# Seven block products for eight in the second projections of a hybrid encoder step, values included

## The chip, the cores and the metric

The kernel runs on one core of a Trainium2 chip. The metric is the device time of one execution in microseconds (us). TensorE (PE) multiplies matrices into PSUM banks; VectorE (DVE), ScalarE (ACT) and GpSimd (POOL) work on tiles in SBUF and PSUM; SyncE (SP) issues DMA transfers. Each engine takes its own instructions in order and waits on semaphores for the others.

## The reference

One inference step of a two-layer streaming encoder on 2048 prompt tokens and 32 sampled tokens (2080 rows, 1024 channels). Layer A is a gated delta rule with its output projection and a layer norm. Its result h goes into the second projections: shared keys and values, queries and gates. Layer B is sliding-window attention with sinks over two earlier chunks of 64 and the own one, gated, projected and normed.

```python
def shared_kv(h, w_kv, pos):
    b, l, _ = h.shape
    kv = h @ w_kv          # 256 key and 256 value channels; the keys are rotated
...
proj = h @ w_in            # 1024 query and 1024 gate channels; the queries are rotated
...
x1 * cos - x2 * sin, x2 * cos + x1 * sin   # on 16 of the 64 channels of a head
```

All products are computed to nearly float32 accuracy from two parts of each operand: hi is the value rounded to the fast matmul format (fp32r), lo = value - hi, and a product is hi x hi + hi x lo + lo x hi.

## The kernel before

The program runs, in order: the projections of layer A, the delta rule, the output projection of layer A (O1, 17 tiles of 128 tokens, which writes h and its transpose hT to DRAM and is in part mixed into the delta rule), the second projections (class P2), and attention with layer B's output projection and norm. This document is about P2, which lies from about 1290 to 1781 us, and the first iterations of attention, which follow.

P2 cuts the 2080 tokens into five blocks of TB = 416 and the channels into tiles ("slabs") of 128. Weights are the stationary operand, activations the moving one. For a slab and a block, `project` issues 24 matmuls of 128x416 into one bank: eight k of 128 input channels by the three hi/lo pairs. Eighteen slabs are projected so: two of keys, eight of queries, eight of gates (z). A slab's weights are loaded by SP (512 KB), rounded to w_hi by ACT, and the rest w_lo is made by POOL (128x1024, line 56). An activation block is loaded in four parts, rounded by ACT (line 70) and its lo made by POOL or DVE (line 71), once for the whole stage; all five blocks stay in SBUF.

Values are computed the other way round, with tokens as stationary operand, since attention wants tokens on partitions: `value_tile` takes 17 tiles of tokens with 24 matmuls of 256 columns each (lines 1389 to 1391).

`rotated` does keys and queries. After each of its 50 blocks come a copy by ACT (line 1345), a stream shuffle by DVE (1346), the product with the sines by POOL (1347) and two DVE operations (1348, 1349). The cosines and sines of all tokens stay in SBUF. Beside it, `keep_out_weights` splits layer B's output weights part by part (lines 1089 to 1093) and stores both parts in DRAM for attention. `gate` makes z/2 and tanh(z/2) on ACT (1430, 1431) and (tanh + 1) z/2 on DVE (1432).

Six or more PSUM banks serve P2 in turn, so that a bank comes free long before it is written again. In P2 only PE's and DVE's order is written by hand, in its first part; the rest is scheduled from the order of the code. Eight gates of blocks 0 and 1 are kept for the start of attention: sixteen halves of twelve matmuls that fill PE's pauses there (`gates`, line 2054 on). Attention takes the score tiles of the prompt in the order 14 to 31, then 0 to 13.

Of the kernel before, what the change touches and what calls it, by code (L numbers as in the profile page):

```python
# [11 lines left out]
F32 = mybir.dt.float32  # L12
# [9 lines left out]
D = 1024  # L22
# [1057 lines left out]
def keep_out_weights(nc, pool, src, kept):  # L1080


    w = D // 2
    last = None
    for k in range(KC):
        for c in (slice(0, w), slice(w, D)):
            t = pool.tile([128, 2, w], F32R, tag="wo_parts", name="wo_parts")
            raw = t[:, 1].bitcast(F32)
            nc.sync.dma_start(raw, src[k][:, c])
            if last:  # L1090
                nc.sync.dma_start(*last)
            nc.scalar.copy(t[:, 0], raw)
            nc.gpsimd.tensor_tensor(out=t[:, 1], in0=raw, in1=t[:, 0], op=ALU.subtract)
            last = kept[:, k, :, c].rearrange("a p d -> p a d"), t[:].bitcast(F32)
            yield
    nc.sync.dma_start(*last)
    yield


# [192 lines left out]
class P2:  # L1292
# [3 lines left out]
    def __init__(self, tc, right, spare, I, O, T):  # L1296
        self.tc, self.nc, self.I, self.O, self.T = tc, tc.nc, I, O, T
        self.resr = new_pool(tc, right, "p2_resr", 1, side="right")
        self.wp = new_pool(tc, right, "p2_w", 2, side="right")
        self.wk = new_pool(tc, right, "p2_wk", 3, side="right")  # L1300
        self.front = ExitStack()
        self.resf = new_pool(tc, self.front, "p2_resf", 1, side="right")
        self.stg = new_pool(tc, spare, "p2_stg", 2, side="right")
        self.ppr = new_pool(tc, spare, "p2_psr", 2, PSUM, side="right")
        self.ppl = None
        self.turn = 0
        self.x = {}
        self.w = {}

    def load_right(self):  # L1310
        for b in (0, 1):
            self.load(b, (self.resf, self.resr)[b])

    def open_left(self, left):
        self.resl = new_pool(self.tc, left, "p2_resl", 1, side="left")
        self.wo = new_pool(self.tc, left, "p2_wo", 2, side="left")
        self.ppl = new_pool(self.tc, left, "p2_psl", 6, PSUM, side="left")
        for b in (2, 3, 4):
            self.load(b, self.resl)

    def load(self, b, res):
        nc = self.nc
        raws = []
        for q in range(4):
            raw = self.stg.tile([128, 2, TB], F32, tag="act_raw", name="act_raw")
            s = slice(q * 2, q * 2 + 2)
            (nc.sync if q % 2 == 0 else nc.scalar).dma_start(
                raw[:], self.T["hT"][s, :, b * TB:(b + 1) * TB].rearrange("h p t -> p h t"))
            raws.append((s, raw[:]))
        self.x[b] = split_acts(nc, res, b, raws, nc.gpsimd if b < 3 else nc.vector)  # L1330

    def ps(self):
        self.turn += 1
        pool = self.ppr if self.ppl is None or self.turn % 4 == 0 else self.ppl
        return pool.tile([128, 512], F32, tag="ps", name="ps")

    def right_ps(self):
        return self.ppr.tile([128, 512], F32, tag="ps", name="ps")

    def rope(self, ps, b, scale):  # L1340
        nc, V = self.nc, self.nc.vector
        ts = slice(b * TB, b * TB + TB)
        a = self.wk.tile([128, TB], F32, tag="ra", name="ra")
        s = self.wk.tile([128, TB], F32, tag="rs", name="rs")
        nc.scalar.activation(a[:], ps, AF.Copy, scale=scale)
        V.stream_shuffle(s[:], a[:], [(i + 8) % 16 if i < 16 else i for i in range(32)])  # L1346
        nc.gpsimd.tensor_tensor(out=s[:], in0=s[:], in1=self.sin[:, ts], op=ALU.mult)  # L1347
        V.tensor_tensor(out=a[:], in0=a[:], in1=self.cos[:, ts], op=ALU.mult)
        V.tensor_tensor(out=a[:], in0=a[:], in1=s[:], op=ALU.add)
        return a  # L1350

    def values(self):
        nc = self.nc
        vh = self.resl.tile([128, KC, 256], F32R, tag="cos", name="vh")
        vl = self.resl.tile([128, KC, 256], F32R, tag="sin", name="vl")
        for i in range(2):
            ks = slice(i * 4, i * 4 + 4)
            vr = self.wp.tile([128, 4, 256], F32, tag="w_raw", name="vr", bufs=1)
            nc.scalar.dma_start(vr[:], self.I["w_v"][:, ks, :])
            nc.scalar.copy(vh[:, ks], vr[:])  # L1360
            nc.gpsimd.tensor_tensor(out=vl[:, ks], in0=vr[:], in1=vh[:, ks], op=ALU.subtract)
        full = TB // 128 * 128
        rows = TB - full
        eh, el = (self.wo.tile([128, 2, D // 2], F32R, tag="wo_parts", name="x_rest")[:].rearrange(
            "p a (b t) -> p (a b) t", t=128) for _ in range(2))
        for b in range(NB - 1):
# [28 lines left out]
    def rotated(self):  # L1395
# [6 lines left out]
        for i in range(10):  # L1402
            w = split_weights(nc, self.wp, I["w_k"][i] if i < 2 else I["b_w_in"][i - 2], nc.gpsimd)
            for b in range(NB):
                if b % 2 == 0:
                    next(beside, None)
# [843 lines left out]
```

## Time and profile before

| | |
|---|---|
| median of the 3 runs shown | 2108.95 us (2107.36 to 2113.84) |
| span of the profiled execution | 2109.4 us |
| PE busy | 2075.3 us, 98% |
| DVE, ACT, POOL busy | 1308.9, 902.1, 833.9 us |
| bytes moved by DMA | 307.78 MB, 146 GB/s |

Share of the span says how much of the time an engine had something to do. The chain that ended last is followed back from the last instruction, at each step to what released it; a share there says what the end depended on. A window's row lists, for a stretch of the span, the busy time of each engine with its instructions, the clock that PE was granted (1.00 is full speed), the share of time in which the 16 DMA engines were busy, and GB/s. A row of the timeline gives start and duration, engine, line, operation, out<-in with their shapes, and in brackets the idle time before and what ended it. A group's row of one line ends with "busy us, mean ns of one | idle time before them".

### The profile page before, as it was taken

The numbers are of one execution on the slowest core, as the hardware profiler recorded it, in microseconds if no ns is written. First come the engines' busy times: TensorE is split into PE (matmuls) and PEld (weight loads), VectorE is DVE, ScalarE is ACT, GpSimd is POOL, SyncE is SP. The second block draws the span as 40 slices with busy tenths as digits, with TensorE's granted clock in tenths as the row PEclk, the third lists the DMA queues.
The fourth block names the chain that finished last, engine by engine and source line by source line (L and its number), as shares of the span: only waits on it lengthen the run. The fifth ranks groups of instructions, "written<-read, shape, count | busy, mean of one in ns | idle before, by whom it ended". The sixth has DMA issues, their size and how long they took to land.

```text
span 2109.4 us, 37222 instructions
## 1 busy us (share of the span) xinstructions
PE 2075.3 (98%) x14062; PEld 1910.6 (91%) x14062; DVE 1308.9 (62%) x2450; ACT 902.1 (43%) x2266; POOL 833.9 (40%) x1180
## 2 busy tenths in 40 slices
PE   8999999999999999999999999999999999999998
PEld 6999999999999999999888888999999997777775
DVE  4676676666557688889977886214544214666665
ACT  4444444445632377667752212312111225555552
POOL 1422222222132187778830201226443103566665
PEclk9999999999999999999999999999999999999999
DMA  5222332346665545556746764546212249534321
GB/s 206 71 62 87 106 111 93 95 127 207 196 195 156 179 157 179 163 169 209 267 162 200 227 213 121 159 154 230 90 66 82 67 109 317 141 101 121 101 72 65
DMA packets 263779, 307.78 MB, mean 146 GB/s; under 512 B 71424, under 2 KB 194624, under 8 KB 263328
## 3 DMA queue, kind: packets, MB, share of 16 engines
q1 hardware_dynamic: 252816, 282.30, 42.8%
q10 hardware_dynamic: 10784, 23.11, 3.3%
q8 instruction: 111, 1.82, 0.4%
q14 instruction: 68, 0.56, 0.1%
HBM read 189.11 MB, written 116.60 MB: 145 GB/s over the span
## 4 chain that ended last, share of the span: by engine, by line
PE 91%; DVE 3%; DMA 2%; POOL 2%; ACT 1%; issue 1%; SPq 0%; DVEq 0%; ACTq 0%; POOLq 0%
PE ps L79 17%; PE ps L81 17%; PE ps L80 17%; PE ot L1146 3%; PE ot L1147 3%; PE ot L1148 3%; PE po L1146 3%; PE po L1148 3%; PE po L1147 3%; PE S L1706 2%; PE ot L1739 2%; PE tr L1721 2%; PE g L695 1%; PE gq L831 1%; PE ks L846 1%; PE sp L846 1%
## 5 line engine op out<-in xcount | busy, mean ns | idle before, releaser
L79 PE MATMUL ps<-act_hi,w_hi 128*128 128x416 f32 x1936 | 682.6, 353 | 0.5 <-ACT act_hi L70 0.4
L81 PE MATMUL ps<-act_hi,w_lo 128*128 128x416 f32 x1936 | 681.4, 352 | 0.0
L80 PE MATMUL ps<-act_lo,w_hi 128*128 128x416 f32 x1936 | 678.4, 350 | 0.5 <-DVE act_lo L71 0.4
L79 PEld LDWEIGHTS ps<-act_hi,w_hi 128*128 128x128 f32 x1936 | 363.9, 188 | 5.3 <-ACT act_hi L70 1.2
L80 PEld LDWEIGHTS ps<-act_lo,w_hi 128*128 128x128 f32 x1936 | 363.7, 188 | 5.5 <-DVE act_lo L71 1.2
L81 PEld LDWEIGHTS ps<-act_hi,w_lo 128*128 128x128 f32 x1936 | 363.4, 188 | 3.7 <-DVE w_lo L56 0.4
L56 POOL TENSOR_TENSOR w_lo<-w_raw,w_hi 128x1024 fp32r<-128x1024 f32 x43 | 115.3, 2682 | 477.3 <-ACT w_hi L55 449.2
L209 DVE SCALAR_TENSOR_TENSOR y<-R,convw,y 128x2083 f32<-128x2083 f32 x72 | 182.9, 2542 | 63.8 <-ACT y L206 47.8
L1540 POOL TENSOR_TENSOR P<-e,sm 128x384 f32<-128x384 f32 (+2 forms) x128 | 101.1, 811 | 170.9 <-DVE sm L1530 164.6
L729 POOL TENSOR_TENSOR tm<-L,Tt 128x60 f32<-128x60 f32 (+19 forms) x365 | 133.6, 366 | 81.2 <-issue 40.1
L731 POOL TENSOR_TENSOR Tt<-Tt,tm 128x60 f32<-128x60 f32 (+19 forms) x365 | 138.7, 380 | 28.6
L1526 ACT ACTIVATE e<-S,nm 128x193 f32<-128x193 f32 (+2 forms) x260 | 104.6, 415 | 95.7 <-DVE nm L1521 58.1
L305 ACT COPY R<-ps 128x416 f32<-128x416 f32 (+1 forms) x144 | 60.2, 442 | 106.8 <-PE ps L81 96.0
L1146 PE MATMUL po<-wo_hi,g_hi 128*128 128x512 f32 x256 | 103.6, 405 | 1.0 <-DVE r L1154 0.8
L1146 PE MATMUL ot<-wo,g_hi 128*128 128x512 f32 x256 | 103.7, 405 | 0.0
L1347 POOL TENSOR_TENSOR rs<-rs,sin 128x416 f32<-128x416 f32 x50 | 70.6, 1412 | 78.8 <-DVE rs L1346 72.6
L1147 PE MATMUL ot<-wo,g_hi 128*128 128x512 f32 x256 | 101.2, 395 | 0.0
L1148 PE MATMUL ot<-wo,g_lo 128*128 128x512 f32 x256 | 101.0, 394 | 0.0
L1148 PE MATMUL po<-wo_hi,g_lo 128*128 128x512 f32 x256 | 100.2, 392 | 0.6 <-DVE g_lo L1189 0.6
L1147 PE MATMUL po<-wo_lo,g_hi 128*128 128x512 f32 x256 | 99.9, 390 | 0.0
L55 ACT CAST w_hi<-w_raw 128x1024 fp32r<-128x1024 f32 x47 | 49.4, 1050 | 108.4 <-PE ps L80 74.3
L1432 DVE SCALAR_TENSOR_TENSOR za<-zs,za 128x416 f32<-128x416 f32 x40 | 31.7, 796 | 102.3 <-ACT za L1431 102.1
(301 smaller groups left out, 3917.9 us busy)
## 6 DMA issues: line engine op xcount, KB each, us to landing
w_raw<-in_w_in SPq DMA_DIRECT2D x40, 512.0 KB
w_raw<-in_b_w_in SPq DMA_DIRECT2D x19, 512.0 KB
k<-s_k SPq DMA_DIRECT2D x17, 512.0 KB
E<-s_E SPq DMA_DIRECT2D x17, 512.0 KB
s_bz<-za SPq DMA_DIRECT2D x40, 208.0 KB
s_bq<-ra SPq DMA_DIRECT2D x40, 208.0 KB
s_q<-y SPq DMA_DIRECT2D x8, 1024.0 KB
s_wo<-wo_parts SPq DMA_DIRECT2D x16, 512.0 KB
```

What stands on the lines that cost most here:

```text
L56: sub.tensor_tensor(out=lo[:], in0=raw[:], in1=hi[:], op=ALU.subtract)
L79: nc.tensor.matmul(ps, hi[:, k, :], xh[:, k, :], start=(k == 0), stop=False)
L80: nc.tensor.matmul(ps, hi[:, k, :], xl[:, k, :], start=False, stop=False)
L81: nc.tensor.matmul(ps, lo[:, k, :], xh[:, k, :], start=False, stop=(k == KC - 1))
L209: nc.vector.scalar_tensor_tensor(out=y[:], in0=R[:, j:j + W], scalar=self.convw[:, i, j:j + 1], in1=y[:], op0=ALU.mult, op1=ALU.add)
L729: P.tensor_tensor(out=tm[:n, i0 - k:, :w], in0=L[:n, i0:, j:j + 1].to_broadcast(sh), in1=Tt[:n, j:j + 1, :w].to_broadcast(sh), op=ALU.mult)
L731: P.tensor_tensor(out=Tt[:n, i0:, :w], in0=Tt[:n, i0:, :w], in1=tm[:n, i0 - k:, :w], op=ALU.subtract)
L1146: nc.tensor.matmul(ps[:n], ghi[:, k, :n], hi, start=a, stop=False)
L1147: nc.tensor.matmul(ps[:n], ghi[:, k, :n], lo, start=False, stop=False)
L1148: nc.tensor.matmul(ps[:n], glo[:, k, :n], hi, start=False, stop=z)
L1526: self.nc.scalar.activation(x.e[:, h, u, :x.n], x.S[:, h, u, :], AF.Exp, bias=x.nm[:, h, u:u + 1], scale=1.0, accum_out=x.sm[:, h, u:u + 1])
L1540: self.nc.gpsimd.tensor_tensor(out=x.P[:, u, :nj * 128].rearrange("r (j h k) -> r j h k", h=2, k=64), in0=x.e[:, :, u, :n].rearrange("r h ...
```

## The change

The second projections are regrouped into 20 feature tiles in ten pairs: keys 0 and 1, values 2 and 3, queries 4 to 11, gates 12 to 19. Block 0 is multiplied as before, but in two products of four k each ("singles", twelve matmuls). Blocks 1 and 2, then blocks 3 and 4, are taken as a 2 x 2 matrix of blocks (halves of k by the two blocks) against 2 x 2 weights (tiles i and i+1 by halves of k), with seven products P1 to P7 of twelve matmuls instead of eight (Winograd's form).

- The seven activation operands b11, b21, t2, t1, t3, t4, b22 are made by `build`, once for each pair of blocks: per k four loads of 208 KB, four sums on POOL, seven roundings on ACT and seven subtractions on DVE. It takes three of its steps after each product while singles run, and what is left before the first paired product.
- The weight operands r1, r2, s1, s2 and two differences are made by `sevens` with four POOL sums per tile pair; each operand of 128x512 is rounded by ACT, and its lo is made by DVE (by POOL until O1 ends). A product's weights are made four products ahead and fetched eight ahead, in a ring of eight slots.
- The sums of products stand in PSUM: P1, then P6, P7 and P4 add up in bank X (two buffers; copied by ACT at each step), P2 in Y, P5 then P3 in Z (one buffer each). DVE adds Y and Z to the copies (line 1447).
- Values come as feature tiles and are turned on PE by 40 transposes (`turn`).
- Weight columns are arranged so that the rotated channels lie in tiles 0, 4 and 8 alone: 15 rotations. Cosines and sines are loaded for each (cs, 416 KB, one buffer). Rows are put back in order by a store to a DRAM scratch (`rows`) and copies from there.
- `out_weights` takes a part of layer B's output weights every seven paired products, with one buffer.
- Every engine's order is now written by hand after O1. Attention takes its tiles from 8 on instead of 14, and has fourteen products of gates (tiles 13 to 19 of block 0) as filler. `LATE` becomes 5.

```diff
+    def part(self, raw, hi, lo, sub):
+        self.nc.scalar.copy(hi, raw)
+        sub.tensor_tensor(out=lo, in0=raw, in1=hi, op=ALU.subtract)
...
+    def sevens(self, raws):
+        r1, r2 = raws
+        a, b = slice(0, 4), slice(4, 8)
+        P = self.nc.gpsimd
+        yield self.operand(r1[:, a])
+        yield self.operand(r1[:, b])
+        s1, s2 = (self.sums.tile([128, 4, 128], F32, tag=t, name=t) for t in ("s1", "s2"))
+        P.tensor_tensor(out=s1[:], in0=r2[:, a], in1=r2[:, b], op=ALU.add)
+        P.tensor_tensor(out=s2[:], in0=s1[:], in1=r1[:, a], op=ALU.subtract)
+        yield self.operand(s2[:])
+        yield self.operand(s1[:])
...
+        for k in range(4):
+            def part(name, raw, sub):
+                self.part(raw[:], x[name][0][:, k, :], x[name][1][:, k, :], sub)
+            b11, b12, b22, b21 = (self.raw_act(i, b) for i, b in ((k, c), (k, d), (4 + k, d), (4 + k, c)))
+            part("b11", b11, nc.vector)
+            yield
+            P.tensor_tensor(out=b11[:], in0=b12[:], in1=b11[:], op=ALU.subtract)
+            part("b21", b21, nc.vector)
+            yield
+            part("b22", b22, nc.vector)
+            P.tensor_tensor(out=b12[:], in0=b22[:], in1=b12[:], op=ALU.subtract)
+            yield
+            P.tensor_tensor(out=b22[:], in0=b22[:], in1=b11[:], op=ALU.subtract)
+            part("t1", b11, nc.vector)
+            yield
+            P.tensor_tensor(out=b21[:], in0=b21[:], in1=b22[:], op=ALU.subtract)
+            part("t2", b22, nc.vector)
...
+        steps = {"P1": ("b11", "X", True, lambda: copied("X", "p1")),
+                 "P2": ("b21", "Y", True, lambda: self.finish(added("Y", "p1"), i, c)),
+                 "P6": ("t2", "X", False, lambda: copied("X", "u2")),
+                 "P5": ("t1", "Z", True, None),
+                 "P7": ("t3", "X", False, after7),
+                 "P4": ("t4", "X", False, lambda: self.finish(copied("X", "c"), i + 1, c)),
+                 "P3": ("b22", "Z", False, lambda: self.finish(added("Z", "u2"), i, d))}
...
+            if last:
+                out += [g["P1"], last["P4"], g["P2"], last["P3"]]
+            else:
+                out += [g["P1"], g["P2"]]
+            out += [g["P6"], g["P5"], g["P7"]]
...
+        early = [*singles(first, self.ps), *one, between[0], a4, between[1], a3, *between[2:], *two, last[0], b4, last[1], b3]
+        late = singles(range(self.Z + 1, self.Z + 8), late_ps)
...
+            if products[p].paired:
+                drain(self.side)
+                next(self.beside, None)
+            yield from self.multiply(products[p])
+            if products[p].after:
+                products[p].after()
+            for _ in range(self.STEPS):
+                next(self.side, None)
...
+        cs = self.tab.tile([128, 2, TB], F32, tag="cs", name="cs")
+        nc.sync.dma_start(cs[:], self.I["cs"][b])
+        s = self.out()
+        V.stream_shuffle(s[:n], a[:n], [(i + 8) % 16 + i // 16 * 16 for i in range(32)])
+        nc.gpsimd.tensor_tensor(out=s[:n], in0=s[:n], in1=cs[:n, 1, :], op=ALU.mult)
+        V.tensor_tensor(out=a[:n], in0=a[:n], in1=cs[:n, 0, :], op=ALU.mult)
+        V.tensor_tensor(out=a[:n], in0=a[:n], in1=s[:n], op=ALU.add)
...
-        order = list(range(14, 32)) + list(range(14))
+        order = list(range(8, 32)) + list(range(8))
```

In the rows below the changed kernel's lines have its own numbers. The first place is right after O1. On POOL there stood, before, the lo parts of block 2, the value weights and the first slabs of keys:

```order
L71 TENSOR_TENSOR act_lo2_13727<-act_raw_13722,act_hi2_13726 128x832
L71 TENSOR_TENSOR act_lo2_13727<-act_raw_13724,act_hi2_13726 128x832
L1370 COPY x_rest_14001<-act_lo2_13727 128x8x32
L1361 TENSOR_TENSOR vl_13991<-vr_13996,vh_13990 128x1024
L1370 COPY x_rest_14001<-act_lo3_13745 128x8x32
L56 TENSOR_TENSOR w_lo_14496<-w_raw_14493,w_hi_14495 128x1024
```

On POOL now stand the sums of the first build (lines 1372 to 1381, one set of four for each k) and the weight sums s1 and s2 of the first pair:

```order
L1372 TENSOR_TENSOR act_raw_13859<-act_raw_13861,act_raw_13859 128x416
L1376 TENSOR_TENSOR act_raw_13861<-act_raw_13863,act_raw_13861 128x416
L1378 TENSOR_TENSOR act_raw_13863<-act_raw_13863,act_raw_13859 128x416
L1381 TENSOR_TENSOR act_raw_13865<-act_raw_13865,act_raw_13863 128x416
L1372 TENSOR_TENSOR act_raw_13944<-act_raw_13946,act_raw_13944 128x416
L1376 TENSOR_TENSOR act_raw_13946<-act_raw_13948,act_raw_13946 128x416
L1347 TENSOR_TENSOR s1_13962<-w_raw_13767 128x512
L1348 TENSOR_TENSOR s2_13963<-s1_13962,w_raw_13765 128x512
L1378 TENSOR_TENSOR act_raw_13948<-act_raw_13948,act_raw_13944 128x416
```

and on DVE, at the same place, the lo parts of the seven operands of the third k, the b11 of the fourth, and weight operands between them:

```order
L1320 TENSOR_TENSOR b11l_13783<-act_raw_13944,b11h_13782 128x416
L1320 TENSOR_TENSOR b21l_13785<-act_raw_13950,b21h_13784 128x416
L1320 TENSOR_TENSOR b22l_13795<-act_raw_13948,b22h_13794 128x416
L1320 TENSOR_TENSOR w_lo_13967<-s2_13963,w_hi_13966 128x512
L1320 TENSOR_TENSOR t1l_13789<-act_raw_13944,t1h_13788 128x416
L1320 TENSOR_TENSOR t2l_13787<-act_raw_13948,t2h_13786 128x416
L1320 TENSOR_TENSOR t3l_13791<-act_raw_13946,t3h_13790 128x416
L1320 TENSOR_TENSOR w_lo_13992<-s1_13962,w_hi_13991 128x512
L1320 TENSOR_TENSOR t4l_13793<-act_raw_13950,t4h_13792 128x416
L1320 TENSOR_TENSOR b11l_13783<-act_raw_14011,b11h_13782 128x416
```

where DVE had gate products and the lo parts of block 3, four of 832 elements:

```order
L1432 SCALAR_TENSOR_TENSOR za_13829<-zs_13830,za_13829 128x416
L1432 SCALAR_TENSOR_TENSOR za_13860<-zs_13861,za_13860 128x416
L71 TENSOR_TENSOR act_lo3_13745<-act_raw_13738,act_hi3_13744 128x832
L71 TENSOR_TENSOR act_lo3_13745<-act_raw_13740,act_hi3_13744 128x832
L71 TENSOR_TENSOR act_lo3_13745<-act_raw_13742,act_hi3_13744 128x832
```

So the subtractions and the sums of a build now stand on the two engines side by side, in many small operations that read two SBUF tiles each.

The second place is the rotation of a query tile. Before, DVE went from one rotation to the next, with banks to spare:

```order
L1346 STREAM_SHUFFLE rs_15091<-ra_15090 128x416
L1348 TENSOR_TENSOR ra_15090<-ra_15090,cos_14489 128x416
L1349 TENSOR_TENSOR ra_15090<-ra_15090,rs_15091 128x416
L1346 STREAM_SHUFFLE rs_15124<-ra_15123 128x416
L1348 TENSOR_TENSOR ra_15123<-ra_15123,cos_14489 128x416
```

Now, for tile 8 of blocks 1 and 2, it stands between the reading of bank Y (P2 of this pair) and that of bank Z (P3 of the pair before):

```order
L1447 SCALAR_TENSOR_TENSOR o_14668<-Y_14699,o_14668 128x416
L1621 STREAM_SHUFFLE o_14715<-o_14668 128x416
L1623 TENSOR_TENSOR o_14668<-o_14668,cs_14713 128x416
L1624 TENSOR_TENSOR o_14668<-o_14668,o_14715 128x416
L1320 TENSOR_TENSOR w_lo_14722<-w_raw_14626,w_hi_14721 128x512
L1447 SCALAR_TENSOR_TENSOR o_14599<-Z_14606,o_14599 128x416
```

and SP, which before had only stores and weight parts there, has the table's load behind the store of one weight part and the load of the next into the same buffer:

```order
L1567 DMA s_wob_65<-wo_parts_14542 128x2x512
L1614 DMA s_bq_73<-s_rows_76 8x16x416
L1610 DMA s_rows_76<-o_14642 128x416
L1565 DMA wo_parts_14697<-in_b_w_out 128x512
L1619 DMA cs_14713<-in_cs 128x832
L1614 DMA s_bq_73<-s_rows_76 8x16x416
```

The reading of Z has moved behind a rotation that waits for a load.

More of the change, by code (lines that the diff above doesn't have):

```diff
@@ L1310, in load_right @@
-    def load_right(self):
-        for b in (0, 1):
-            self.load(b, (self.resf, self.resr)[b])
-    def open_left(self, left):
[L1315 to L1330, printed above, removed]
+        self.ident = G["ident"]
@@ L1332, in ps, with go @@
+    def go(self, n):
+        for _ in range(n):
+            self.left -= 1
+            yield next(self.main)
     def ps(self):
[L1333 to L1337, printed above, removed]
         return self.ppr.tile([128, 512], F32, tag="ps", name="ps")
-    def rope(self, ps, b, scale):
-        nc, V = self.nc, self.nc.vector
[L1342 to L1350, printed above, removed]
@@ L2173, in host_inputs @@
     ang = inv[:, None] * pos[None, :]
[L2174 to L2179 removed]
+    cos, sin = np.cos(ang), np.sin(ang)
+    both = np.stack([np.tile(np.concatenate([cos, cos]), (8, 1)), np.tile(np.concatenate([-sin, sin]), (8, 1))], 1)
+    out["cs"] = c(both.reshape(128, 2, NB, TB).transpose(2, 0, 1, 3))
     q = np.arange(128) % 32
```

443 lines of the change are left out of this document (270 added, 173 removed).

## The prediction

> **What bounds the kernel now.** I read the page's busy shares first, then the chain that ended last, then windows of the second-projection stretch, PE's waits in it, and last single rows of VectorE (DVE) and GpSimd (POOL).
>
> ```profile
> span 2109.4 us, 37222 instructions
> PE 2075.3 (98%) x14062; PEld 1910.6 (91%) x14062; DVE 1308.9 (62%) x2450; ACT 902.1 (43%) x2266; POOL 833.9 (40%) x1180
> PE 91%; DVE 3%; DMA 2%; POOL 2%; ACT 1%; issue 1%; SPq 0%; DVEq 0%; ACTq 0%; POOLq 0%
> 1327.60:1395.30 67.70, 67.06 (x505) 65.46 (x503) 13.69 (x14) 18.93 (x37) 6.23 (x4) 1.00 0.37 117
> 1410.00:1640.00 230.00, 230.00 (x1218) 228.13 (x1217) 105.56 (x196) 44.42 (x78) 110.03 (x73) 1.00 0.35 120
> 1725.50:1781.00 55.50, 53.39 (x376) 46.59 (x374) 22.28 (x42) 28.67 (x101) 12.95 (x16) 1.00 1.01 293
> ```
>
> TensorE (PE) is busy 98% of the span and carries 91% of the chain. In a window's row stand its length, then busy time and count of PE, PEld, DVE, ACT and POOL, PE's clock, the DMA share and GB/s. From 1410 to 1640 PE isn't idle at all: 1218 matmuls of 416 columns take 230.00 us, **0.1889 us each**, and a product of twelve 2.27 us. So a matmul taken away here is worth its full time, and any new wait of PE is paid in full. DVE and POOL are each under half busy there, which will matter when they get more to do at one place.
>
> **What goes.** Counted over the program, the matmuls with 416 columns are 6000 before and 6000 after: the eighth saved on blocks 1 to 4 is just what the values cost as feature tiles. What PE loses is the old value matmuls. They all lie in the window from 1327.6:
>
> ```profile
> L80 PE MATMUL ps<-act_lo,w_hi 128*128 128x416 f32 x32 | 11.6, 362 | 0.5 <-DVE act_lo L71 0.4
> L81 PE MATMUL ps<-act_hi,w_lo 128*128 128x416 f32 x32 | 11.2, 351 | 0.0
> L79 PE MATMUL ps<-act_hi,w_hi 128*128 128x416 f32 x33 | 10.8, 363 | 0.5 <-ACT act_hi L70 0.4
> L1721 PE MATMUL tr<-ident,P 128*128 128x128 f32 x66 | 9.3, 277 | 0.0
> PE ot L79 <- ACT w_hi L55: 1.5, 1, 1.5
> PE ot L81 <- DVE w_lo L56: 0.6, 1, 0.6
> PE ps L80 <- DVE act_lo L71: 0.4, 1, 0.4
> PE ps L79 <- ACT act_hi L70: 0.4, 1, 0.4
> ```
>
> Of its 505 matmuls 32 + 32 + 33 = 97 are gates, so 408 are values: 67.06 - 97 x 0.1889 = **48.7 us gone**. Added are 40 transposes; 66 of a like size took 9.3 us, 0.14 each: **+5.6**. The four waits in the last rows, 2.9 us together, belong to the old activation loads and old late slabs, and go: **-2.9**. With every new wait hidden the kernel would take 2109.4 - 48.7 + 5.6 - 2.9 = **2063.4**. Everything below is added to that.
>
> **The two builds.** Blocks 1 and 2, later 3 and 4, need seven operands with 28 casts (ACT), 28 subtractions (DVE) and 16 sums (POOL). These start when O1 ends, and again when the last product of the first pair of blocks is done; eight single products of block 0 cover each, 8 x 2.27 = 18.1 us. P1 then reaches its fourth k after nine more matmuls, 19.8 us after the start. DVE and POOL are not free of each other:
>
> ```profile
> 70.31 2.40 POOL L56 TENSOR_TENSOR w_lo<-w_raw,w_hi 128x1024 fp32r<-128x1024 f32 x1 [32.44 <-ACT w_hi L55]
> 78.75 13.38 POOL L56 TENSOR_TENSOR w_lo<-w_raw,w_hi 128x1024 fp32r<-128x1024 f32 x1 [0.88 <-POOL convo L203]
> 87.35 2.37 DVE L209 SCALAR_TENSOR_TENSOR y<-R,convw,y 128x2083 f32<-128x2083 f32 x1
> ...
> 1423.43 1.30 POOL L1093 TENSOR_TENSOR wo_parts<-wo_parts 128x512 fp32r<-128x512 f32 x1 [0.62 <-ACT wo_parts L1092]
> 1424.69 2.40 POOL L56 TENSOR_TENSOR w_lo<-w_raw,w_hi 128x1024 fp32r<-128x1024 f32 x1
> 1425.42 2.12 DVE L1348 TENSOR_TENSOR ra<-ra,cos 128x416 f32<-128x416 f32 x1
> 1428.52 0.59 DVE L1349 TENSOR_TENSOR ra<-ra,rs 128x416 f32<-128x416 f32 x1 [0.97 <-POOL rs L1347]
> L56 DVE TENSOR_TENSOR w_lo<-w_raw,w_hi 128x1024 fp32r<-128x1024 f32 x3 | 3.7, 1225 | 12.7 <-ACT w_hi L55 12.7
> ```
>
> The POOL subtraction that takes 2.40 us alone took 13.38 when DVE was at its own work: DVE's L209 ended at 89.72, and 2.40 after that is 92.12, just where POOL ended. The other way round, DVE's L1348 lasted 2.12 for 0.59, ending at 1427.54, 0.45 after POOL's 2.40 were over at 1427.09. So a subtraction or sum of two SBUF tiles on one engine waits for such a one on the other, but for some 0.14 us at a change of hands. By the rows, ahead of P1's fourth k stand on DVE 22 subtractions of 416 (0.59 each, 13.0) and 7 of 512 weight columns (half of 1.225, 4.3), on POOL 12 sums of 416 (1.30 x 416/512 = 1.06 each, 12.7) and 2 of 512 (2.6): 32.6 us in one line, less some 26 changes at 0.14, 3.6, makes 29.0. Against 19.8 that is a wait of 9.2 us; t2 for the third product after P1 needs five or six rows more in the same line and may add 2. If the two engines didn't hinder each other, DVE's 17.3 would fit, with a wait of 1 at most for the last cast. If nothing is gained at the changes and the first operations come late behind O1's, 12.8 + 2 + 1 = 16. **Build 1: +9 (1 to 16).** Build 2 has the same line and a rotation (POOL 1.06 to 1.43, DVE 2 x 0.59: about 2.4) in front, one more before t2: **+12 (1 to 20).**
>
> The Trainium skill bears on this place. Its page "SBUF — State Buffer", section "Who interferes with whom", says that a VectorE instruction with two SBUF inputs contends with a GpSimd one that reads SBUF, the first to start keeping the port pair for the whole instruction. The rows agree but for the 0.14 at the hand-over; by the page the wait of build 1 would be 32.6 - 19.8 = 12.8 and by the rows 9.2.
>
> A long wait of PE can also cost clock afterwards:
>
> ```profile
> 1028.00:1030.00 2.00, 1.18 (x10) 1.21 (x11) 0.48 (x2) 0.00 (x0) 1.69 (x5) 1.00 0.86 331
> 1030.00:1032.00 2.00, 2.00 (x21) 2.00 (x20) 1.80 (x3) 0.40 (x1) 1.61 (x6) 1.00 0.07 27
> ...
> 1060.00:1062.00 2.00, 0.17 (x10) 0.17 (x12) 1.86 (x7) 0.46 (x1) 1.61 (x6) 1.00 0.89 331
> 1062.00:1064.00 2.00, 2.00 (x38) 1.94 (x34) 2.00 (x8) 1.25 (x4) 1.61 (x6) 0.55 0.04 11
> 1064.00:1066.00 2.00, 2.00 (x13) 2.00 (x12) 1.41 (x3) 1.58 (x10) 1.61 (x6) 0.60 0.74 244
> ```
>
> After an idle stretch of about 2 us (0.17 busy of 2.00) the clock was 0.55 and 0.60 for 4 us, a loss of 2 x 0.45 + 2 x 0.40 = 1.7; after a like one around 1028 it stayed at 1.00. Two long waits, 0 to 1.7 each: **+3 (0 to 3.4).** By the Trainium skill, "TensorE: Matmul & The Clock Gate", Part 1, it takes an idle window of about 3.4 us to halve the clock, which only the builds' waits would fill; the row with 2 us says less can be enough.
>
> **Rotations in the paired stretch.** Fifty rotations become fifteen, but a rotation now stands on DVE between two products that share a bank. When P2 of tiles 4 and 8 ends (T), DVE adds its product, shuffles, multiplies, adds, makes a w_lo, and only then reads bank Z of the pair before, which P5, two products after P2, writes again at T + 4.5.
>
> ```profile
> 1424.75 0.63 DVE L1346 STREAM_SHUFFLE rs<-ra 128x416 f32<-128x416 f32 x1
> 1315.39 3.51 DMA act_raw<-s_hT
> 1322.02 4.22 DMA act_raw<-s_hT
> 1427.05 1.43 POOL L1347 TENSOR_TENSOR rs<-rs,sin 128x416 f32<-128x416 f32 x1
> L1430 ACT ACTIVATE zs<-ps 128x416 f32<-128x416 f32 x32 | 16.5, 516 | 75.9 <-PE ps L81 75.9
> ```
>
> No row shows DVE adding a PSUM bank of this width; I take 0.6 for it, by the 0.59 of 416 elements. With the table there in time: 0.6 + 0.63 + 1.43 (one wait for the other engine in it) + 0.59 + 0.61 + 0.6, and 0.7 for one more such wait, are 5.2: some 0.6 late. But the table is now fetched for each use, 416 KB, the size that took 3.51 and 4.22 us in this trace, and its DMA stands on SP behind a weight load that waits for the store before it. Landing at T + 3.5, it makes DVE 2.6 late. Four such places (tiles 4 and 8, both pairs of blocks), 0.6 to 2.6 each; I take the middle: **+7 (2 to 10).**
>
> **Attention.** Sixteen halves of gates filled PE's pauses in its first iterations; now fourteen products of the same size do. Two halves, 24 matmuls, are missing: at most 24 x 0.1889 = 4.5 us of cover, and nothing if PE's own work is as long as the softmax chain there. Key and weight loads come in the same stretch, which already moves 293 GB/s at a DMA share of 1.01, so the upper end is set at 6: **+2 (0 to 6).** The order of loads around O1's end: 0 (-1.5 to 1.5), as the same bytes are fetched there earlier. In the steady stretch seven products give 15.9 us; a Z pair needs in the DVE/POOL line 7 x 0.61 + 4 x 0.59 + 5 x 1.30 = 13.2, which fits; ACT's casts and copies, the 80 weight sums on POOL and the 60 additions from PSUM have their cover there. So have 50 more stores and as many bytes copied back in DRAM: some 21 MB in about 450 us, 47 GB/s beside the 120 at a DMA share of 0.35. **0**, and what it costs if the line doesn't fit is the second rival.
>
> **Sum:** 2063.4 + 9 + 12 + 3 + 7 + 2 = **2096 us**, against the span of 2109.4 of the profiled execution. The median of the runs shown, 2108.95, is 0.5 below it, so no correction is made for what lies around the span.
>
> **Rivals.**
> *The builds are covered.* If DVE's and POOL's operations interlock less than the 2.12 and 13.38 rows say, builds cost 2 together, no clock, rotations 4, attention 2: 2071. For it: not every such pair is long (0.59 at 1428.52, begun when POOL had ended). Against it: in a build both queues are full.
> *Every group waits: slower.* Bank Z has one buffer. If in each of the twenty groups of seven the read of Z by DVE comes late behind a two-tile operation that waits for POOL (1.30 for a weight sum, 2.6 for two), as it does in my rotations, P5 waits in every group. It decides from (2115.7 - 2096)/20 = 1.0 us per group on; with 1.3, 2122. For it: in Z tiles an ACT tanh and a two-tile DVE product stand ahead of that read (0.6 + 0.52 + 0.59 + 0.61 + 1.3 + 0.6 = 4.2 of 4.5). Against it: PE needs 15.9 and the line 13.2 at worst, 10.8 for Q.
> *The loads bound the builds.* A build fetches sixteen parts of 208 KB, and beside them up to eight weight tiles of 512 KB: 7.6 MB, at the 293 GB/s of the row from 1725.5 some 26 us for a cover of 19.8. If the line can't run while it lacks them, that is up to 6 more at each build: 2108, no difference.
> *The change doesn't do what it says*: excluded as to the matmul counts, which the order shows.
>
> **Chances.** About 0.3%, 6 us, is what a measurement of this kernel can tell from no change: faster is below 2103, slower above 2115.5. Forecast (2085 to 2105) 0.51, of which 0.08 lies within 0.3%; builds covered (2063 to 2085) 0.20; loads (2103 to 2115) 0.14; every group waits 0.15. Faster 0.43 + 0.20 = 0.63, same 0.22, slower 0.15. The range goes from build costs at their lower ends (2063.4 + 1 + 1 + 2 = 2067) to the upper (2063.4 + 16 + 20 + 3.4 + 10 + 6 = 2119, cut to 2118 as all ends together are unlikely); it leaves out most of the slower case and little else.
>
> **What would show it.** Right: PE busy near 2032 us plus stretches at half clock; one PE wait of some 9 us after O1 and one of some 12 in mid-stretch, both at P1's fourth k, released by DVE's b11 rows; DVE rows of 0.59 lasting 1.6 to 2 there; four waits of P5 on DVE's read of Z of 0.6 to 2.6. Wrong: PE released there by a DMA or ACT, builds without a wait, or waits in every group. The sum fails most easily in the builds, where 29 us of work stand against 20 of cover.

## The result, and the profile after

| | before | changed |
|---|---|---|
| median of the runs shown | 2109.24 us (4 runs) | 2182.91 us (4 runs) |
| ratio, 95% interval | | 1.0338 (1.0316 to 1.036), slower |
| span of the profiled execution | 2109.4 us | 2174.9 us (2176.69 as timed) |
| PE busy | 2075.3 us | 2058.8 us |

The forecast was 2096, faster. The kernel became 3.4% slower. All sums below are made against the profiled execution, the fastest of the four.

The page of the changed kernel, with its busy shares and its chain:

```profile
span 2174.9 us, 37101 instructions
PE 2058.8 (95%) x13694; PEld 1886.2 (87%) x13694; DVE 1429.6 (66%) x2585; ACT 993.6 (46%) x2466; POOL 886.9 (41%) x1239
PE 76%; POOL 7%; DMA 6%; issue 5%; DVE 3%; ACT 1%; SPq 1%; ACTq 0%; POOLq 0%; DVEq 0%
```

Its waits of PE by line (us in total, times, longest us):

```profile
PE Z L1576 <- DVE o L1447: 44.7, 12, 8.4
PE X L1576 <- ACT b11h L1319: 14.9, 3, 8.6
PE X L1576 <- ACT o L1442: 12.2, 2, 8.0
PE tr L1928 <- POOL P L1747: 7.7, 4, 4.4
PE tp L1630 <- ACT o L1412: 3.7, 1, 3.7
PE tp L1630 <- ACT v L1632: 2.8, 1, 2.8
PE X L1577 <- DVE b11l L1320: 1.2, 2, 1.0
```

PE's share of the chain fell from 91% to 76%. The places of the waits are those that the prediction named (P1 and t2 at the builds, Z behind rotations) and three it had put at nothing or little (Z in gate groups, the turns `tp`, attention's `tr`). Read one by one from PE's gaps, the new waits are, in us:

| where | forecast | measured |
|---|---|---|
| build 1 (P1's k's, then t2) | 9 | 8.6 + 1.0 + 4.2 = 13.7 |
| build 2 | 12 | 5.9 + 8.1 = 13.9 |
| Z behind the four rotations | 7 | 8.3 + 7.9 + 7.7 + 8.4 = 32.3 |
| Z in gate groups | 0 | 1.5 + 3 x 2.5 + 2.1 + 0.6 + 0.6 = 12.3 |
| turns of the values | 0 | 3.8 + 2.8 = 6.5 |
| attention's opening | 2 | 4.4 + 2.6 + 0.6 = 7.6 |
| clock | 3 | 26.6 |

The clock's row comes from PE's busy time: 2075.3 - 48.7 + 5.6 = 2032.2 was due by the counted work, 2058.8 is there, 26.6 more for the same matmuls; the mean clock granted was 0.978, and 0.998 before. How that looks is seen behind two equal waits of 2.51 us at gate groups, in windows (length, busy time and count of PE, PEld, DVE, ACT, POOL, clock, DMA share, GB/s):

```profile
1489.00:1491.40 2.40, 0.04 (x1) 0.07 (x1) 1.70 (x3) 1.14 (x3) 0.00 (x0) 1.00 0.27 104
1491.40:1494.80 3.40, 3.40 (x18) 3.38 (x19) 2.50 (x4) 2.36 (x5) 0.00 (x0) 1.00 0.23 79
...
1507.50:1510.00 2.50, 0.03 (x1) 0.06 (x1) 1.71 (x4) 1.20 (x3) 0.00 (x0) 1.00 0.31 117
1510.00:1513.40 3.40, 3.40 (x12) 3.26 (x13) 2.50 (x4) 2.36 (x5) 0.00 (x0) 0.60 0.20 76
```

PE is called busy in both stretches of 3.40 us, but in the second it finishes 12 matmuls and not 18. A busy share hides this: the count beside it shows it. From P2 on in the changed kernel every wait of 2.6 us or more was followed by such a stretch, two of the three waits of 2.5, and no single one under 2.1. Behind a long wait the stretch can last longer: from 1436.8 to 1442.4, after 7.9 us for Z, PE was busy throughout and finished 16 matmuls in 5.6 us at a clock of 0.50. The 14 dips cost 1.4 to 2.8 us each.

Forecast's base and the measured rows add up: 2063.4 + 13.7 + 13.9 + 32.3 + 12.3 + 6.5 + 7.6 + 26.6 = 2176.3, against 2174.9.

The largest row is one chain at each of four places. Here it is at tile 4 of blocks 1 and 2, first in the chain of waits (start, us, what):

```profile
1379.78 6.91 DMA s_wob<-wo_parts
...
1386.70 0.34 SPq L1565
1387.04 0.05 issue
1387.10 3.66 DMA cs<-in_cs
...
1390.89 1.48 POOL o L1622
```

and in DVE's timeline (start, us, engine, line, operation):

```profile
1385.08 0.58 DVE L1447 SCALAR_TENSOR_TENSOR o<-Y,o 128x416 f32<-128x416 f32 x1
1385.70 0.62 DVE L1621 STREAM_SHUFFLE o<-o 128x416 f32<-128x416 f32 x1
1390.85 0.59 DVE L1623 TENSOR_TENSOR o<-o,cs 128x416 f32<-128x416 f32 x1 [4.52 <-DMA cs<-in_cs]
1392.39 1.63 DVE L1624 TENSOR_TENSOR o<-o 128x416 f32<-128x416 f32 x1 [0.95 <-POOL o L1622]
1394.55 0.58 DVE L1447 SCALAR_TENSOR_TENSOR o<-Z,o 128x416 f32<-128x416 f32 x1
```

SP stands until the store of a weight part has landed, 6.91 us after its issue, since the next part has the same buffer; only then come that part's load and the table's, which takes 3.66. DVE stands 4.52 for the table, and Z is read at 1394.55. P5 had been ready since 1395.19 - 8.30 = 1386.89. P2's last matmul ended at 1381.64, two products and some transposes before that. So the table, there at 1390.76, landed 9.1 us after P2's end, where I had set 3.5 as the worst. DVE was also 3.4 us late with Y before it began, behind w_lo operations of the weight sums.

At build 1 PE was released by ACT, at P1's fourth k by the rounding of b11 and at t2 by the copy of bank X. ACT's rows:

```profile
1334.89 0.62 ACT L1319 CAST w_hi<-s 128x512 fp32r<-128x512 f32 x1 [5.06 <-POOL s L1348]
1338.15 0.54 ACT L1319 CAST b11h<-act_raw 128x416 fp32r<-128x416 f32 x1
1346.70 0.54 ACT L1319 CAST t2h<-act_raw 128x416 fp32r<-128x416 f32 x1 [2.01 <-POOL act_raw L1378]
1348.29 0.51 ACT L1442 ACTIVATE o<-X 128x416 f32<-128x416 f32 x1
```

ACT takes its work in order, so what it waits for on POOL holds back the roundings and the copy behind.

### The profile page after: what moved, and what is told of

It is laid out like the page before. It is cut to its first block, busy times and chain, and to the rows that moved or that the text cites. A ratio compares the mean times of both kernels' runs of the same rounds, so it can differ in the third digit from the quotient of the medians.

```text
span 2174.9 us, 37101 instructions
## 1 busy us (share of the span) xinstructions
PE 2058.8 (95%) x13694; PEld 1886.2 (87%) x13694; DVE 1429.6 (66%) x2585; ACT 993.6 (46%) x2466; POOL 886.9 (41%) x1239
## 4 chain that ended last, share of the span: by engine, by line
PE 76%; POOL 7%; DMA 6%; issue 5%; DVE 3%; ACT 1%; SPq 1%; ACTq 0%; POOLq 0%; DVEq 0%
PE ps L79 11%; PE ps L81 11%; PE ps L80 11%; PE ot L1126 3%; PE ot L1128 3%; PE ot L1127 3%; PE po L1126 3%; PE po L1128 3%; PE po L1127 2%; PE S L1913 2%; PE ot L1946 2%; PE tr L1928 2%; POOL tm L729 2%; POOL Tt L731 2%; DMA s_wob<-wo_parts 2%
## 5 line engine op out<-in xcount | busy, mean ns | idle before, releaser
L79 PE MATMUL ps<-act_hi,w_hi 128*128 128x416 f32 x1280 | 452.8, 354 | 0.0
L81 PE MATMUL ps<-act_hi,w_lo 128*128 128x416 f32 x1280 | 450.7, 353 | 0.0
L80 PE MATMUL ps<-act_lo,w_hi 128*128 128x416 f32 x1280 | 447.9, 350 | 0.0
L80 PEld LDWEIGHTS ps<-act_lo,w_hi 128*128 128x128 f32 x1280 | 240.5, 188 | 3.5
L79 PEld LDWEIGHTS ps<-act_hi,w_hi 128*128 128x128 f32 x1280 | 240.4, 188 | 3.2 <-issue 0.4
L81 PEld LDWEIGHTS ps<-act_hi,w_lo 128*128 128x128 f32 x1280 | 240.2, 188 | 2.1
L56 POOL TENSOR_TENSOR w_lo<-w_raw,w_hi 128x1024 fp32r<-128x1024 f32 x25 | 71.5, 2861 | 320.3 <-ACT w_hi L55 292.4
L1320 DVE TENSOR_TENSOR w_lo<-w_raw,w_hi 128x512 fp32r<-128x512 f32 x130 | 95.2, 755 | 34.3 <-ACT w_hi L1319 33.1
L1319 ACT CAST w_hi<-w_raw 128x512 fp32r<-128x512 f32 x140 | 81.6, 617 | 46.8 <-POOL w_raw L1354 29.6
L1320 DVE TENSOR_TENSOR w_lo<-s,w_hi 128x512 fp32r<-128x512 f32 x40 | 38.9, 1000 | 72.1 <-ACT w_hi L1319 72.1
```

Source lines behind the costliest of these rows:

```text
L79: nc.tensor.matmul(ps, hi[:, k, :], xh[:, k, :], start=(k == 0), stop=False)
L80: nc.tensor.matmul(ps, hi[:, k, :], xl[:, k, :], start=False, stop=False)
L81: nc.tensor.matmul(ps, lo[:, k, :], xh[:, k, :], start=False, stop=(k == KC - 1))
L1320: sub.tensor_tensor(out=lo, in0=raw, in1=hi, op=ALU.subtract)
```

## The experiments

Time is that of a run or the median of runs; "span" is that of the profiled execution. The kernel before ran on the same chip with each set, at 2107.6 to 2111.3. Where no interval is given, an edit ran once; runs of the kernel before lay up to 7 us apart (2106.8 to 2113.4), so a smaller step in time is read from the waits alone.

### The order on DVE, the weight part's buffer, the gates

Three edits, alone and together. The rotation is taken out of DVE's way:

```diff
+        self.delay(lambda: self.spin(a, n, cs), 1)
+
+    def spin(self, a, n, cs):
+        nc, V = self.nc, self.nc.vector
         s = self.out()
         V.stream_shuffle(s[:n], a[:n], ...
```

> The rotation's shuffle, products and sum are issued one product later, behind DVE's read of bank Z; its table load stays where it is. Theory (order on DVE makes the four long waits of Z, 8.3 + 7.9 + 7.7 + 8.4 = 32.3 us in the changed kernel): these four fall under 1 us each, and with the clock that they cost the span falls by some 35 to 40, to about 2135 to 2140. Rival (the table's late load is the bottleneck wherever it stands): the weight parts now queue behind the rotation on DVE and PE waits for those instead, 4 to 8 us at each place, span over 2155.

Measured: 2169.9, span 2168.1, 7 less and not 35. The four waits of Z went, but P4 waited for bank X instead (3.6 + 1.6 + 1.5 + 3.5) and the turns 13 more. At the first of the waits for X DVE's timeline reads

```profile
1451.63 0.59 DVE L1627 TENSOR_TENSOR o<-o,cs 128x416 f32<-128x416 f32 x1 [5.79 <-DMA cs<-in_cs]
```

and ACT's

```profile
1454.40 0.62 ACT L1319 CAST w_hi<-w_raw 128x512 fp32r<-128x512 f32 x1 [8.78 <-POOL w_raw L1354]
1454.93 0.51 ACT L1442 ACTIVATE o<-X 128x416 f32<-128x416 f32 x1
```

POOL, in order, holds the rotation's product in front of the fourth weight sum (L1354); ACT stands 8.78 us for that sum, and behind it is the copy that frees X. The table's lateness went through another engine's queue. The rival was nearer, though it named the wrong queue: it was not w_lo on DVE.

```diff
-                t = self.tab.tile([128, 2, w], F32R, tag="wo", name="wo_parts")
+                t = self.tab.tile([128, 2, w], F32R, tag="wo", name="wo_parts", bufs=2)
```

> Two buffers for a part of the output weights instead of one, so that the load of the next part and the table behind it don't wait for the store. Theory (SP stands for 6.9 us at the landing of that store, and the table behind it): the four long waits of Z shrink from 8 to 1 to 2.6 us each; the waits of 1.5 to 2.5 at the gate groups shrink too, because POOL no longer sits 11 us in front of the weight sums; span 2135 to 2150. Rival (the order on DVE alone): the gate groups keep their waits of 2.5, span over 2150.

Measured: 2164.5, span 2162.7. The four waits became 4.5 + 4.8 + 4.7 + 5.7 = 19.6: 12.7 less, a gain of the right kind, and half of what was expected. SP no longer stood, but the table (issued at 1381.16, behind two loads of 512 KB, a store of 512 KB and a part of 256 KB) still came 7 us later. DVE's 2.1 us for it and POOL's product are what is left at 1388.63:

```profile
1381.16 0.98 SPq L1619 DMA_DIRECT2D cs<-in_cs  x1
...
1388.63 0.59 DVE L1623 TENSOR_TENSOR o<-o,cs 128x416 f32<-128x416 f32 x1 [2.10 <-DMA cs<-in_cs]
```

The gate groups kept their 2.51, so POOL's wait there isn't for that load.

```diff
-            nc.vector.scalar_tensor_tensor(out=c[:], in0=t[:], scalar=1.0, ...)
+            self.delay(lambda: nc.vector.scalar_tensor_tensor(out=c[:], in0=t[:], scalar=1.0, ...), 1)
```

> Only the gate tiles' product with tanh is issued one product later, behind the read of Z. Theory (the gate groups' waits, 1.45 + 3 x 2.51 + 2.06 + 0.59 + 0.64 = 12.3 us, come from ACT's tanh in front of that read): they fall to under 3 together, span some 2160. Rival (they come from POOL, whose weight sums stand behind a late part of the output weights, and DVE's w_lo behind those): they shrink by 1 us each at most and the span stays over 2167.

Measured: 2184.0, span 2182.1: no gain. The three waits of 2.51 stayed to the hundredth; in blocks 3 and 4 the two of 0.6 went. The tanh in front of the read of Z is not what makes the larger ones.

> The three edits together. If the Z waits are all that these edits touch, 32 + 12 us of waits and about 12 us of clock go: span some 2118 to 2125, still above the kernel before, since the two builds (27.6 us), the turns (6.5) and attention (7) keep theirs.

Measured: 2149.1, ratio 1.018 (1.015 to 1.021), span 2146.5, 28 less than the changed kernel, where 50 to 57 were expected: the gate waits were still there, and PE's busy time was 2058.0, so the clock's loss was too. It serves as the base of the next set.

### What the gate groups, the builds and the clock wait for

The weight part's subtraction on POOL comes five products later:

```diff
-  ...t[:, 0], t[:, 1], nc.gpsimd), 4)    ...t[:].bitcast(F32)), 6)
+  ...t[:, 0], t[:, 1], nc.gpsimd), 9)    ...t[:].bitcast(F32)), 11)
```

> On top of the three edits: the output-weight part's rounding and subtraction come five products later in a group (after nine products instead of four, its store after eleven instead of six), so that POOL takes it behind the next pair's weight sums and not in front. Theory (the gate groups' waits of 2.51 each come from POOL's order: the weight sums stand behind that subtraction, DVE's w_lo behind them, the read of Z behind those): the 7.5 us of Z waits fall under 2, span 2136 to 2142. Rival (they come from DVE's own load in a gate group): they stay at 2.5 each and the span within 3 us of 2146.

Measured: 2156.5, span 2154.7. The 7.5 us of Z waits went to nothing, as the theory of POOL's order had it, but P4 waited 5.0, 2.5, 5.0 and 2.6 for X and the turns more: the store, five products later, now landed after the load that needs its buffer was due, and SP stood again in front of a table. The mechanism held and the span's forecast missed.

The sums of both builds on VectorE:

```diff
-        nc, P = self.nc, self.nc.gpsimd
+        nc, P = self.nc, self.nc.vector
```

> On top of the three edits: the 32 sums of the two builds on VectorE instead of GpSimd. Theory (the builds are one line of DVE and POOL operations that exclude each other, and a sum is 0.6 on DVE against 1.06 to 1.4 on POOL): build 1's waits, 8.54 + 1.00 + 4.04, fall to 6 to 9 in all, build 2's 5.29 + 6.26 likewise, span 2133 to 2139. Rival (DVE and POOL work side by side, DVE's own work is then the bound): DVE gets 9.4 us more at each build and the waits grow by 5 or more each, span over 2152. Second rival (loads or ACT's order bound the builds): no change.

Measured: 2137.4, span 2135.6, 10.9 less than the base. Build 1's waits fell from 13.6 to 5.4 (5.0 + 0.5), build 2's from 11.6 to 6.4 (1.3 + 5.1), although DVE got all 32 sums of the builds. If the two had worked side by side, DVE's own work would have grown past the cover and the waits with it. Rows of the changed kernel's build 1, which the base shares, show a reason, on POOL and DVE:

```profile
1329.55 1.39 POOL L1372 TENSOR_TENSOR act_raw<-act_raw 128x416 f32<-128x416 f32 x1 [2.64 <-DVE b11l L1320]
1329.93 1.45 DVE L1320 TENSOR_TENSOR b22l<-act_raw,b22h 128x416 fp32r<-128x416 f32 x1
1335.54 0.89 DVE L1320 TENSOR_TENSOR w_lo<-s,w_hi 128x512 fp32r<-128x512 f32 x1 [4.16 <-ACT w_hi L1319]
1336.35 1.45 DVE L1320 TENSOR_TENSOR t1l<-act_raw,t1h 128x416 fp32r<-128x416 f32 x1
```

and these of build 2 with the sums on DVE:

```profile
1541.45 0.59 DVE L1320 TENSOR_TENSOR b11l<-act_raw,b11h 128x416 fp32r<-128x416 f32 x1
1541.95 0.69 DVE L1320 TENSOR_TENSOR w_lo<-w_raw,w_hi 128x512 fp32r<-128x512 f32 x1
1542.56 0.59 DVE L1372 TENSOR_TENSOR act_raw<-act_raw 128x416 f32<-128x416 f32 x1
1543.06 0.59 DVE L1320 TENSOR_TENSOR b21l<-act_raw,b21h 128x416 fp32r<-128x416 f32 x1
```

In the first a subtraction takes 1.45 beside a sum of 1.39 on POOL; in the second, with POOL out of the way, both take 0.59. How much of the gain is the end of the blocking, and how much the cheaper sum and the handing over between engines that went with it, this run doesn't tell apart. The Trainium skill's "SBUF — State Buffer", section "Who interferes with whom", says that a VectorE instruction with two SBUF inputs contends with a GpSimd instruction that reads SBUF, and calls the shared port pair an exclusive lock. The rows agree, with 1.45 against 0.59.

Useless matmuls in PE's waits:

```diff
             if products[p].paired:
                 drain(self.side)
+                for _ in range(self.pad):          # 3 at each build
+                    self.idle_product(products[p]) # twelve matmuls into a spare bank, read by nobody
```

> On top of the three edits: three products of twelve matmuls whose result is used by nobody, 6.8 us of PE work, in front of the first paired product of each build, where PE waits 8.5 and 5.3 us. Theory (a wait of PE of 3 us and more halves the clock for 3.4 us, and costs 1.7 and more by that): PE's waits there fall to about 2 and 0, the clock after them stays at 1.00 at build 1, and the span does not grow, it falls by 0 to 4 although 13.6 us of work were added (build 2 may pay up to 1.5 for work that doesn't fit its wait). Rival (the clock falls for other reasons, as by the power drawn): no change of the clock after build 1, span the same or longer by 1 to 3.

Measured: 2148.8, span 2146.6 with 72 matmuls (13.6 us) more, 2146.5 without. The stretch at build 1 in the base, in windows:

```profile
1330.00:1340.00 10.00, 1.11 (x3) 0.49 (x3) 5.84 (x8) 4.87 (x11) 7.53 (x6) 0.74 0.27 87
1340.00:1345.00 5.00, 3.85 (x10) 3.29 (x11) 2.93 (x5) 1.05 (x3) 3.11 (x3) 0.50 0.86 228
```

and with the idle products:

```profile
1330.00:1340.00 10.00, 8.75 (x43) 7.63 (x42) 5.76 (x8) 4.27 (x10) 7.13 (x7) 1.00 0.42 130
1340.00:1345.00 5.00, 2.81 (x13) 2.19 (x13) 4.49 (x8) 3.26 (x7) 1.86 (x2) 1.00 0.31 83
```

The clock stayed at 1.00 while PE was kept at work, so the wait is what lowers it; the rival is out. PE's busy time grew by 6.7 us for 13.6 of work (2058.0 to 2064.7). But the span didn't fall: t2's wait grew from 4.0 to 5.5. While other engines bound a build, a PE at full clock only waits longer. So a dip inside a build was no loss here; at gate groups, where PE is the bound behind it, it should be one, but no run tried useless matmuls there.

> Both the later weight part and the sums on VectorE on top of the three edits: by the first theory of each, span 2124 to 2132, still above the kernel before by some 15 to 20; what is left are the builds, the turns of the values and attention's opening with their clock.

Measured: 2140.8, span 2139.0: 3.4 above b1 and not below it. The waits of Z went again, but P4 waited 19.4 us in all for X, where the late phase alone had made 15.1 of it.

### Towards a version that keeps the gain

```diff
-        v = self.tab.tile([128, 4, 128], F32, tag="v", name="v")
+        v = self.tab.tile([128, 4, 128], F32, tag="v", name="v", bufs=2)
-        nc.gpsimd.tensor_tensor(out=s[:n], in0=s[:n], in1=cs[:n, 1, :], op=ALU.mult)
+        V.tensor_tensor(out=s[:n], in0=s[:n], in1=cs[:n, 1, :], op=ALU.mult)
```

> On top of the three edits and the sums on VectorE: two buffers for a turned value tile, so that ACT's copy doesn't wait 6.3 us for the store of the one before, and the rotation's product with the sines on VectorE, so that DVE doesn't wait for POOL in it. Theory (the turns wait for that store, and build 2's waits of 1.3 + 5.1 come from two rotations in which DVE stands 3.5 us for POOL each): the waits of the transposes fall from 11.8 to under 6 in all, build 2's from 6.4 to under 3, span from 2136 to 2122 to 2128. Rival (the build's line is full without the rotations): build 2 keeps its 6, span over 2130.

Measured: 2117.2, span 2115.4, 20 less than b1. The turns' waits fell from 11.8 to 7.3 (6.0 + 1.3), a little short of the forecast; build 2's stayed at 6.0, so the rotations in it were not its bound. The gain is larger than these waits: X's wait of 1.1 behind a rotation went, the gate groups' fell a little (12.5 to 11.2), and PE's busy time fell from 2056.9 to 2046.6, as dips of the clock went with the waits. That POOL's sums no longer stand behind a table fits this, but wasn't tried by itself.

```diff
-  ... nc.gpsimd), 4)    ... t[:].bitcast(F32)), 6)
+  ... nc.gpsimd), 7)    ... t[:].bitcast(F32)), 9)
```

> As c1_turns_and_rotations, and the weight part's subtraction stands on POOL between the third and fourth weight sum (after seven products instead of four, store after nine instead of six). In p1_weight_part_phase the gate groups' Z waits went but SP stood 6 us for a store that landed too late; here the store is two products earlier. Theory (POOL's order makes the gate waits): the waits of 2.2 to 2.8 at the gate groups, 12.5 in all, go, no new ones of over 3 come, span 8 to 15 below c1. Rival (any place of this part costs a wait somewhere): other waits take their place, span within 4 of c1.

Measured: 2111.0, span 2109.2, 6.2 below c1, a little short of the 8 expected. The gate groups' Z waits are gone (11.2 to 0.7), so POOL's order made them: in the changed kernel POOL stood 34.8 us in four places of that stretch for the part's rounding, with the weight sums of the next pair behind it:

```profile
POOL wo_parts L1320 <- ACT wo_parts L1319: 34.8, 4, 11.7
```

Build 2's t2 now waits 7.8 where it waited 3.6, and build 1's 3.7 where it waited 0.7, which takes back part of it.

```diff
-    LOOK, FETCH, DELAY, STEPS = 4, 4, 2, 3
+    LOOK, FETCH, DELAY, STEPS = 4, 4, 2, 4
```

> As c2_weight_part_between, with four steps of a build after each product instead of three. Theory (the build is a full line of DVE from its first step): no change of its wait of 5 us, span within 2 of c2. Rival (ACT's order, in which a step stands behind the copy of a single's bank, holds the build back): the wait falls by 2 to 4.

Measured: 2102.0, span 2100.2, 9.0 below c2. Build 1's first wait fell from 5.7 to 2.8 and its t2's from 3.7 to 2.3; build 2's 1.1 + 7.8 went, and two turns' waits of 3.3 + 3.9 became 5.4 + 5.1. So with the sums on DVE the line isn't full: ACT's order, where a build's rounding stands behind the copy of a single's bank, held it back. My theory fell there, the rival held.

```diff
-            self.delay(lambda: self.turn(c, i - self.V, b))
+            self.delay(lambda: self.turn(c, i - self.V, b), 5 if b == 0 else None)
```

> As c3_four_steps, and the two value tiles of block 0 are turned five products after their last matmul instead of two. Theory (PE waits 5.4 + 5.1 us for them in build 2 because ACT, in order, is behind with the build's casts, and nothing else needs the turned tiles): both waits go, with one or two dips of the clock, span 2086 to 2092, time 1% below the kernel before. Rival (the build's line then holds P1 of blocks 3 and 4 back by as much): build 2 gets 6 to 10 us of waits instead, span 2097 to 2101, half a per cent below or less.

Measured: median 2100.8 against 2109.2, ratio **0.9962 (0.9948 to 0.9976)**, span 2097.7: 0.4% less than the kernel before, a small gain whose interval leaves out 1, and 3.8% less than the changed kernel. The turns' waits moved rather than went; the waits of PE at build 2 are now

```profile
PE ps L1576 <- ACT o L1412: 7.3, 2, 5.9
PE tp L1635 <- ACT v L1637: 6.2, 1, 6.2
```

of 13.5 in all: a single's bank that ACT has not yet copied, and a turn behind ACT's copy. The rival was right: in build 2 PE waits for ACT's and DVE's work, wherever the program has it wait. The page's row for PE is

```profile
PE 2040.9 (97%) x13694; PEld 1874.6 (89%) x13694; DVE 1452.4 (69%) x2632; ACT 994.9 (47%) x2466; POOL 837.9 (40%) x1192
```

with the same 13694 matmuls as the changed kernel: 17.9 us of busy time less for the same work, some 14 of it by the clock (half of the time that PE was busy at a clock of 0.50: 27.5 us in the changed kernel, 13.5 here).

## Why the prediction was wrong

The step that failed most is the price of the table's landing at the rotations, and next to it the clock, charged to two waits alone. Term by term:

- **What goes** (-48.7 + 5.6 - 2.9): right (230.00/1218 is 0.1888 a matmul and not 0.1889, which moves nothing). c4's busy time comes within 9 of the 2032.2 due, and the bound of 2063.4 plus the measured waits and clock gives the measured span.
- **The builds** (9 and 12): mechanism right in part; sizes 13.7 and 13.9, inside the ranges given. At build 1 the line was sized right: from the first b11's subtraction to the fourth's, 1309.2 to 1340.4, DVE or POOL was at work for 29.0 of 31.2 us, as the sum has it, and P1 waited 8.6 + 1.0 for the 9.2 forecast. That the two hinder each other fits the run with the sums on DVE. Two things went otherwise. PE was released at P1's fourth k by ACT, which I had listed as a sign of being wrong: ACT stood 5.1 us for the weight sum s2, with the build's roundings behind it. And t2, for which I had named 2 and put nothing into the 9, waited 4.2 and 8.1, since the copy of bank X stands on ACT behind the fourth k's roundings.
- **The rotations** (7, 2 to 10): mechanism right, down to the named store, load and table; the size was 32.3. Mis-sized is the table's landing. I set it at most 3.5 us behind P2's end, which is a load's duration alone, without the issue: the store ahead took 6.91 and the table 3.66, and it landed 9.1 behind. I had the row for a 416 KB load and none for a 512 KB store in a loaded queue, and priced the store's landing at nothing, after naming it.
- **The clock** (3, at most 3.4): mechanism right, and mis-sized: 26.6 for 3, the second largest miss. I charged it to two long waits at up to 1.7; nearly every wait of 2.5 us or more pays it, fourteen of fifteen, and each 1.4 to 2.8. The page "TensorE: Matmul & The Clock Gate" of the Trainium skill, Part 1, asks for an idle window of about 3.4 us. The traces differ: here waits of 2.5 did it two times in three, as the row of 2 us in the trace of before had shown could happen.
- **The steady stretch** (0): wrong. I compared sums of busy time, 13.2 (its terms make 13.1) against 15.9, and they did fit. What made P5 wait was the order: a weight part's subtraction in front of the next pair's sums on POOL, whose input came when ACT got to it. That is the second rival's place, bank Z in the groups, with another cause than the tanh I gave it, shown by the runs that moved the tanh (no change) and the part (waits gone). It cost 12.3, not the 20 and more at which that rival would decide.
- **The turns** (5.6 for their work): their waits, 6.5, weren't in the sum; the rows name ACT's copies. A second buffer for them, tried together with another edit, took 4.5 of 11.8 us; ACT's delay in build 2 fits the rest.
- **Attention** (2, 0 to 6): 7.6 with its clock aside, a little over the end given. That its filler is shorter was not tried alone, so the cause stays open: the row names POOL's P, as would fit.
- **The loads** as a rival: no PE wait at a build was put down to a load in the changed kernel. SP's issue of the third and fourth k's loads did wait for free tiles, and build 1's chain, followed back, holds a load of 5.68 us for the third k. That wasn't tried alone, so the loads aren't excluded as a part.
- The sign failed with two terms: 25.3 us too little at the rotations and 23.6 at the clock. Together with 12.3 at the gate groups, and 5.6 to 6.6 each at the builds, the turns and attention, they turn -13 into +65.

## What to carry to other kernels

When a wait is named, follow its chain to the end and price each link in the state it will be in: a store's landing behind other transfers, the issue queue behind the store, the engine in order behind the load. Busy sums of a stretch say that work fits, not that it comes in time: where four engines run in hand-written order, look for the instruction with the latest input and list what stands behind it on its engine. And on a kernel that keeps PE at work without a break, price each new wait of 2.5 us and more with the half clock behind it, if PE is the bound there: here 1.7 us after a wait of 2.5, and up to 2.8 after one of 8.

## What was not expected of the hardware

Waits as short as 2.5 us lowered PE's clock at times, and those from 2.6 us on always in the changed kernel, for 2.8 to 5.6 us of PE's work. Over all the runs there is no sharp limit: of 24 single waits of 2.5 us 17 were followed by half clock, one of 1.56 was (1004.8 in the run of both the later part and the sums), and one of 3.53 wasn't (1693.6 in the run with the rotation behind). Filling two such waits with useless matmuls kept the clock at 1.00 behind them, at no measurable cost in time and without a gain. And the same subtraction of 416 elements takes 0.59 us or 1.45, sums included, by the engine on which its neighbour runs: moving work from a half idle POOL to a busier DVE made the stage faster.
